# Second block's attention scores: split queries and keys in three single passes on each head's own rows

## The chip, the core and the metric

The kernel runs on one core of one Trainium2 chip. The metric is the device time of one execution in microseconds (us); three runs of the kernel before are given, and their median is the time compared. The engines are TensorE (PE, and PEld for its weight loads), VectorE (DVE), ScalarE (ACT), GpSimd (POOL), and SyncE (SP), which issues the DMAs.

## What is computed

A network of two layers of a first block and two layers of a second block acts on 256 tokens of width 1024, all in float32. The change concerns the second block. There a layer normalises its input, multiplies it by one large matrix, and gives the columns to four kinds of attention with four heads each:

```python
# sparse ("dsa"): an indexer of 8 heads of width 64 chooses the keys, then 4 heads of width 64
dots = jnp.einsum('bthd,bsd->bths', iqb, ik)
score = jnp.einsum('bth,bths->bts', iwb, jax.nn.relu(dots))      # the 64 best keys of a query stay
logits = jnp.einsum('bthd,btjhd->bhtj', qb, k_sel) * scale
# forgetting: 4 heads of width 64, a decay is added to the scores
logits = jnp.einsum('bthd,bshd->bhts', qb, k) * scale + decay
# differential: 4 heads with two score maps each, of width 32; out = (p0 - lam * p1) @ v
logits = jnp.einsum('bthmd,bshmd->bmhts', qb, k) * scale
# sliding: 4 heads of width 64, two key heads, window of 128, a sink in the softmax
logits = jnp.einsum('bnikgd,bnjkd->bnkgij', qb, k_win) * scale
```

Each is causal and followed by a softmax and the product with the values. The four outputs, 1024 columns together, go through an output matrix, a normalisation and a residual sum, and then through a feed-forward part.

## The kernel before, in words

Tokens stand in two tiles of 128. Weights are streamed: `convert` (lines 263 to 298) loads a unit of up to 128x1024 values into `raw`, ScalarE copies it to a high part `wh` of type float32r (line 291), and VectorE, or GpSimd for a few units next to a boundary, subtracts that from `raw` to give the rest `wl` (line 294). `mm3` (line 316) then makes each weight product in three single passes on float32r operands: high by high, high by rest, rest by high (lines 320 to 322). A product of plain float32 operands is one call in the code and two MATMUL instructions in the trace, which are called passes here.

The order of work on each engine is found at build time by a scheduler that simulates the program, and is fixed then; each engine takes its instructions in that order. Where the code puts parts of equal standing by turns, it does so with `weave` (line 540).

A layer of the second block is `second_layer`. Its four mixers `dsa` (1408), `differential` (1532), `sliding` (1585) and `forgetting` (1488) are generators, cut into phases at a bare `yield`. `phases` (551) runs them in the order of `RUN2`: the products of dsa, those of differential, the choosing of dsa, the products of sliding, the attention of differential, the products of forgetting, then the attention of dsa, sliding and forgetting. `BANKS` gives each mixer its two banks of PSUM: `pd` for dsa, `pc` for differential, `pa` for forgetting, `acc` for the attention of sliding; `pt` (181) hands them out by turns. `SLOTS` gives it slots of SBUF of three sizes.

Scores are needed per head, while the transposed queries stand with two heads of width 64 (or four of width 32) on the 128 rows of a tile. The kernel before makes an operand per row position: `padded` (1371) takes two or four tiles [128, 2, 256] and has GpSimd fill them with zeros (line 1379); `pad_copy` (1382) has ScalarE copy only the rows of one position into each (line 1385). The keys stay whole, in one tile (`2_qkT`, or `2_iT` for the indexer), copied by ScalarE at lines 1400, 1493 and 1605. A score is then one float32 matmul on all 128 rows, in which the zeros of the query take the other heads' keys out:

```python
for i, h in enumerate(heads):
    nc.tensor.matmul(bv[:, i], qT[h % 2][:, h // 2, t * 128:t * 128 + 128], kT[:, h // 2, :nk], ...)
```

These stand at line 1445 (indexer, in `choose`), 1479 (dsa), 1525 (forgetting), 1568 (differential) and 1617 (sliding). Queries of tile 0 see 128 keys, those of tile 1 see 256, so a score has 128 or 256 columns.

`softmax_av` (578) takes a token tile's four heads in two steps. A step takes one bank, has `scores` fill it for two heads (first the causal mask as a bfloat16 matmul, `causal_mm`, line 636, and in forgetting the decays as float32 matmuls, lines 1522 and 1524; then the scores), takes the maximum on VectorE (line 590), the negative of it (596), and the exponentials with their sums on ScalarE (601); then it yields to the other token tile. After both steps `av` transposes the probabilities (622), copies them (625, 627) and multiplies by the values (633). The first block's attention (`mixer_c`, scores at line 940) uses the same function. One place of the first block, line 1088, has matmuls on 64 of the 128 rows. The mixed outputs are split into high and rest at lines 383 and 384.

Of the kernel before, what the change touches and what calls it, by code (L numbers as in the profile page):

```python
# [11 lines left out]
F = mybir.dt.float32  # L12
# [9 lines left out]
D = 1024  # L22
# [25 lines left out]
# steps of the two token tiles between two products  # L48
# [53 lines left out]
# work slots of a group: (tag, bytes of a partition, count), the smallest that fits is taken  # L102
# [7 lines left out]
# work tiles and banks of the mixers of the second block, in phase one and two  # L110
# [8 lines left out]
# banks of PSUM of a group  # L119
# [11 lines left out]
class K:  # L131
# [57 lines left out]
    def z(self, shape, name, g=None, dt=F, bufs=None):  # L189
        """work tiles of a group of slots"""  # L190
# [16 lines left out]
    def col_load(self, ap, rows, name):  # L207
        """[rows * 128] contiguous values -> [128, rows] (value r * 128 + p at [p, r])."""
# [9 lines left out]
    def rsq(self, ssq, n, mul, add, name="rs"):  # L218
        """(ssq * mul + add) ** -0.5"""
# [33 lines left out]
    def head(self, kind):  # L253
        """the next units may take those slots as well, when what is before the boundary is done"""
# [8 lines left out]
    def convert(self, i, stack):  # L263
# [4 lines left out]
        # the last units of a product before a boundary have slots of their own  # L268
# [13 lines left out]
        # next to a boundary the vector engine has the norms to do, and small pieces let those pass  # L282
# [3 lines left out]
        if near and i >= self.near + first:  # L286
            # the norms of the token tiles go ahead
# [28 lines left out]
    def mm3(self, out, a, b, first, last):  # L316
        """out += (ah + al).T @ (bh + bl)"""
# [6 lines left out]
    def tm(self, xT, *blocks, outs=None):  # L324
        """token-major products: each block (key, tiles of rows in a unit, columns) -> its columns of a bank a token tile"""
# [15 lines left out]
    def fm(self, xT, key, out=None):  # L341
        """feature-major product of 256 columns: [128, 2, 256]"""
# [11 lines left out]
    def fm_early(self, xT, key, banks=("acc", "pc"), out=None):  # L354
        """the same by way of a token-major product, which needs one token tile at a time"""
# [18 lines left out]
    def tsplit(self, src, t, hT, lT, k0, nk):  # L374
        """src [128 tokens, nk * 128] -> transposed and split into hT, lT[:, k0:k0 + nk, token tile t]"""
# [14 lines left out]
    def sum_sq(self, a, b, psum=False):  # L390
        """steps: sum of a ** 2 and b ** 2 over 1024 columns, / 1024 + eps, to the power of -1/2"""
# [19 lines left out]
    def warm(self, x, n):  # L411
        """products of no use: the clock of the tensor engine halves when it rests between two products"""
# [8 lines left out]
    def steps(self, accs, post, pre, xT, t, gated=False, out=None):  # L421
        """x += rms norm of the product in PSUM; rms norm of the residual stream, transposed and split. In steps, which
        are numbered, so that those of the two token tiles can be put in order"""
        nc = self.nc
        xs = self.halves(t)
        if gated:
            for hf, x in enumerate(xs):
                sg = self.z([128, 512], "ny")
                nc.scalar.activation(sg, accs[t][hf], AF.Tanh, scale=0.5)
                yield                                   # 0, 3  # L430
                nc.vector.scalar_tensor_tensor(sg, sg, 1.0, post[t][hf], op0=OP.add, op1=OP.mult)
                yield                                   # 1, 4
# [3 lines left out]
                yield                                   # 2, 5  # L436
        elif accs is not None:
            sq = self.sum_sq(*accs[t], True)
            for _ in range(2):
                next(sq)  # L440
                yield                                   # 0, 1
            ys = [self.z([128, 512], "ny", "N") for _ in range(2)]
            nc.vector.tensor_tensor(ys[0], accs[t][0], post[0], OP.mult)
            yield                                       # 2
            next(sq)
            r = self.r
            yield                                       # 3
            nc.vector.tensor_tensor(ys[1], accs[t][1], post[1], OP.mult)
            yield                                       # 4
            for hf, (y, x) in enumerate(zip(ys, xs)):  # L450
# [3 lines left out]
                yield                                   # 5, 6  # L454
# [12 lines left out]
        for hf in range(2):  # L467
# [35 lines left out]
    def big_out(self, xT, key, order=range(8)):  # L503
        """[256, K] @ [K, 1024] -> 2 x 2 banks"""
# [5 lines left out]
    def down(self, accs, steps, first, last):  # L510
        """the last units go one token tile after the other, so that the first is done early"""
# [27 lines left out]
    @staticmethod  # L539
    def weave(*gens):  # L540
        """steps of independent parts in turn"""
# [9 lines left out]
    def phases(gens, order):  # L551
        """each mixer stands in the order once for each of its phases, the first of which are its products"""
# [25 lines left out]
    def softmax_av(self, t, scores, v, scale, sinkrow=None, raw=False):  # L578
        """Steps. scores(bank, heads): fills PSUM [128, 2, nk] of two heads; v(h, kt): [128, 64]; gives (o PSUM, rs).
        Heads of one row position of the tensor engine share a bank."""  # L580
# [4 lines left out]
        for par in range(2):  # L585
# [1158 lines left out]
```

## Time and profile before

| | us |
|---|---|
| median of three runs | 1544.99 |
| lowest, highest run | 1538.86, 1549.9 |
| the profiled execution: span from first to last instruction | 1548.7 |
| its own time | not given apart; of the three runs the nearest is 1549.9 |
| TensorE busy, of the span | 1494.2 |
| VectorE, ScalarE, GpSimd busy | 1007.5, 827.9, 288.0 |

"Busy" counts the time in which at least one instruction of the engine is under way. Matmuls overlap in the trace (the next starts before the last has drained), so what a matmul costs is read from the distance of the starts, not from the duration. A chain row shows, piece by piece, the work that ended last.

### The profile page before, as it was taken

How to read it: one execution, taken by the hardware profiler on the slowest of the kernel's cores; microseconds unless marked ns; L12 is line 12 of the kernel's file. 1: busy time of each engine (PE TensorE's matmuls, PEld its weight loads, DVE VectorE, ACT ScalarE, POOL GpSimd, SP SyncE). 2: the span in 40 equal slices, each digit the busy share in tenths (PEclk: the TensorE clock that was granted, in tenths of full speed). 3: DMA queues.
4: the chain of work that ended last, by engine and by line, in shares of the span. 5: the costliest groups of instructions: out<-in, count | busy, mean ns of one | idle time of the engine just before them, and what ended most of it. 6: DMA issues, size and time to landing. Idle time of an engine off the chain costs nothing.

```text
span 1548.7 us, 25270 instructions
## 1 busy us (share of the span) xinstructions
PE 1494.2 (96%) x9723; PEld 1337.0 (86%) x9731; DVE 1007.5 (65%) x1737; ACT 827.9 (53%) x1443; POOL 288.0 (19%) x377
## 2 busy tenths in 40 slices
PE   7999999999998999999999999999999999999998
PEld 7978889999896887999978888899977888899996
DVE  6897577556789755656666875554566695654455
ACT  5735456445574534544445674555564575555553
POOL 1554210000255322000033122000014231100010
PEclk9999999999999979999999999999999999999999
DMA  7522246666452213666646343556654543466663
GB/s 236 150 84 83 72 149 189 186 183 198 135 158 79 74 57 111 191 188 181 189 135 191 105 138 116 180 187 190 187 188 135 165 124 109 130 190 188 190 194 109
DMA packets 156422, 234.12 MB, mean 151 GB/s; under 512 B 11700, under 2 KB 118158, under 8 KB 156302
## 3 DMA queue, kind: packets, MB, share of 16 engines
q1 hardware_dynamic: 156302, 232.51, 49.5%
q8 instruction: 76, 1.25, 0.3%
q14 instruction: 44, 0.36, 0.1%
HBM read 231.43 MB, written 1.05 MB: 150 GB/s over the span
## 4 chain that ended last, share of the span: by engine, by line
PE 77%; DVE 12%; ACT 4%; DMA 3%; POOL 2%; issue 2%; SPq 0%; ACTq 0%; DVEq 0%; POOLq 0%
PE acc L322 7%; PE acc L320 7%; PE acc L321 7%; PE pa L320 6%; PE pa L322 6%; PE pa L321 6%; PE pc L320 5%; PE pc L322 5%; PE pc L321 5%; PE pd L322 4%; PE pd L321 4%; PE pd L320 4%; DVE wl L294 3%; DVE gl_r L700 1%; ACT wh L291 1%
## 5 line engine op out<-in xcount | busy, mean ns | idle before, releaser
L294 DVE TENSOR_TENSOR wl<-raw,wh 128x1024 fp32r<-128x1024 f32 (+4 forms) x424 | 485.3, 1152 | 362.8 <-ACT wh L291 361.7
L291 ACT ACTIVATE wh<-raw 128x1024 fp32r<-128x1024 f32 (+4 forms) x420 | 433.2, 1035 | 413.2 <-PE pd L321 100.0
L294 POOL TENSOR_TENSOR wl<-raw,wh 128x1024 fp32r<-128x1024 f32 (+1 forms) x26 | 61.7, 2374 | 647.6 <-ACT wh L291 647.6
L322 PE MATMUL pa<-xTh,wl 128*128 128x256 f32 x512 | 145.5, 284 | 0.0
L320 PE MATMUL pa<-xTh,wh 128*128 128x256 f32 x512 | 145.4, 284 | 0.0
L321 PE MATMUL pa<-xTl,wh 128*128 128x256 f32 x512 | 145.2, 284 | 0.0
L322 PE MATMUL pd<-xTh,wl 128*128 128x256 f32 x432 | 122.4, 283 | 0.5 <-DVE wl L294 0.5
L320 PE MATMUL pd<-xTh,wh 128*128 128x256 f32 x432 | 122.3, 283 | 0.0
L321 PE MATMUL pd<-xTl,wh 128*128 128x256 f32 x432 | 122.2, 283 | 0.0
L320 PEld LDWEIGHTS pa<-xTh,wh 128*128 128x128 f32 x512 | 98.2, 192 | 0.3
L321 PEld LDWEIGHTS pa<-xTl,wh 128*128 128x128 f32 x512 | 98.2, 192 | 0.3
L322 PEld LDWEIGHTS pa<-xTh,wl 128*128 128x128 f32 x512 | 98.1, 192 | 0.2
L320 PEld LDWEIGHTS pd<-xTh,wh 128*128 128x128 f32 x432 | 82.8, 192 | 0.9
L321 PEld LDWEIGHTS pd<-xTl,wh 128*128 128x128 f32 x432 | 82.8, 192 | 0.9
L322 PEld LDWEIGHTS pd<-xTh,wl 128*128 128x128 f32 x432 | 82.8, 192 | 0.8 <-DVE wl L294 0.8
L321 PE MATMUL acc<-wl,f_h 128*128 128x512 f32 x200 | 78.4, 392 | 0.0
L322 PE MATMUL acc<-wh,f_l 128*128 128x512 f32 x200 | 77.3, 390 | 0.6 <-DVE f_l L1259 0.6
L321 PE MATMUL pc<-wl,f_h 128*128 128x512 f32 x200 | 77.8, 389 | 0.0
L322 PE MATMUL pc<-wh,f_l 128*128 128x512 f32 x200 | 77.5, 389 | 0.0
L320 PE MATMUL acc<-wh,xTh 128*128 128x512 f32 (+4 forms) x200 | 71.3, 360 | 1.5 <-ACT xTh L477 1.1
L320 PE MATMUL acc<-wh,f_h 128*128 128x512 f32 x200 | 71.4, 393 | 0.2 <-ACT f_h L1257 0.2
L320 PE MATMUL pc<-wh,f_h 128*128 128x512 f32 x200 | 71.3, 389 | 0.0
(630 smaller groups left out, 3869.8 us busy)
## 6 DMA issues: line engine op xcount, KB each, us to landing
raw<-in_w_in_dram SPq DMA_DIRECT2D x84, 512.0 KB, 3.7
raw<-in_w_mlp_up_dram SPq DMA_DIRECT2D x64, 512.0 KB, 3.8
raw<-in_w_mlp_down_dram SPq DMA_DIRECT2D x64, 512.0 KB, 3.7
raw<-in_ffn_w_gate_dram SPq DMA_DIRECT2D x44, 512.0 KB, 3.8
raw<-in_ffn_w_up_dram SPq DMA_DIRECT2D x44, 512.0 KB, 3.8
raw<-in_ffn_w_down_dram SPq DMA_DIRECT2D x44, 512.0 KB, 3.6
raw<-in_w_out_dram SPq DMA_DIRECT2D x32, 512.0 KB, 3.8
raw<-in_w_ple_gate_dram SPq DMA_DIRECT2D x16, 512.0 KB, 4.3
```

Of the source, the lines that this page charges most:

```text
L291: nc.scalar.activation(h[:, p], raw[:, p], AF.Copy)
L294: e.tensor_tensor(l[:, p], raw[:, p], h[:, p].bitcast(F), OP.subtract)
L320: t.matmul(out, ah, bh, start=first, stop=False, skip_group_check=True)
L321: t.matmul(out, ah, bl, start=False, stop=False, skip_group_check=True)
L322: t.matmul(out, al, bh, start=False, stop=last, skip_group_check=True)
L700: nc.vector.tensor_tensor(R[:, j].rearrange("p h (b s) -> p h b s", s=s), ev[:, ft[j], :, 1][:, None].to_broadcast([128, 2, 128 // s, s]), ...
```

## The change

Each set of queries and keys becomes a pair of float32r tiles, high part and rest (`hl`), made by `split_to`: ScalarE copies the high part from PSUM, VectorE subtracts it from the same PSUM values. The padded operands, their zeros and the copies into them go. A score is three single passes, high by high, high by rest, rest by high, on the 64 (or 32) rows of its own head. `softmax_av` takes both banks at once, and `row_mm` issues the passes of two heads on different row positions by turns, one into each bank; both banks are filled before the softmax of the first begins, and there is one yield for the two. In `choose` the eight heads are ordered the same way, and the heads of a row position share a bank. The probabilities are as wide as the keys. Comments were removed too; they are left out of the diff.

```diff
 def softmax_av(self, t, scores, v, scale, sinkrow=None, raw=False):
...
-        for par in range(2):
+        banks = [self.pt()[:, :2 * nk].rearrange("p (h k) -> p h k", k=nk) for _ in range(2)]
+        scores(banks)
+        for par, bv in enumerate(banks):
             hs = slice(par, 4, 2)
-            bv = self.pt()[:, :2 * nk].rearrange("p (h k) -> p h k", k=nk)
-            scores(bv, (par, par + 2))
...
-            Pp = self.z([128, 2, 256], "sm_p")
+            Pp = self.z([128, 2, nk], "sm_p")
...
-            yield
+        yield
...
+    def row_mm(self, banks, q, k, last=True):
+        for j in range(2):
+            qk = [(q(i, j), k(i, j)) for i in range(2)]
+            for n, (x, y) in enumerate(((0, 0), (0, 1), (1, 0))):
+                for bv, (a, b) in zip(banks, qk):
+                    self.nc.tensor.matmul(bv[:, j], a[x], b[y], start=False, stop=last and n == 2 and j == 1,
+                                          skip_group_check=True)
+    def rows_of(self, w, t, nk, q, k):
+        rr = lambda i: slice(i * w, i * w + w)
+        return (lambda i, j: [x[rr(i), j, t * 128:t * 128 + 128] for x in q], lambda i, j: [x[rr(i), j, :nk] for x in k])
+    def hl(self, n, name):
+        return [self.z([128, n, 256], name, dt=FR) for _ in range(2)]
+    def split_to(self, dst, o, src):
+        h, l = dst
+        self.nc.scalar.activation(h[o], src, AF.Copy)
+        self.nc.vector.tensor_tensor(l[o], src, h.bitcast(F)[o], OP.subtract)
...
 def heads_T(self, src, n, dst, t):
...
-            if isinstance(y, list):
-                self.pad_copy(y, p[:, g:g + m], 128 // len(y), ts)
-            else:
-                nc.scalar.activation(y[:, :m, ts], p[:, g:g + m], AF.Copy)
+            self.split_to(dst[g // 2], (slice(None), slice(0, m), slice(t * 128, t * 128 + 128)), p[:, g:g + m])
...
 def dsa(self, l, xT):
-        qT, kT = qkT = [self.padded(64, "2_qz"), self.z([128, 2, 256], "2_qkT")]
-        iT = [self.padded(64, "2_iz"), self.padded(64, "2_iz"), self.z([128, 2, 256], "2_iT")]
+        qT, kT = qkT = [self.hl(2, "2_qT"), self.hl(2, "2_kT")]
+        iT = [self.hl(2, "2_iq"), self.hl(2, "2_iq"), self.hl(1, "2_ik")]
...
 def choose(t):
-            for h0 in range(0, 8, per):
-                hl = [(h0 + i) * 2 % 8 + (h0 + i) // 4 for i in range(per)]
-                p = self.pt().rearrange("p (h k) -> p h k", k=nk)
-                for i, h in enumerate(hl):
-                    nc.tensor.matmul(p[:, i], iT[h // 4][h % 2][:, h // 2 % 2, t * 128:t * 128 + 128], iT[2][:, 0, :nk],
-                                     start=True, stop=True)
+            rr = lambda i: slice(64 * i, 64 * i + 64)
+            for j0 in range(0, 4, per):
+                banks = [self.pt().rearrange("p (h k) -> p h k", k=nk) for _ in range(2)]
+                for j in range(j0, j0 + per):
+                    for n, (x, y) in enumerate(((0, 0), (0, 1), (1, 0))):
+                        for i, p in enumerate(banks):
+                            nc.tensor.matmul(p[:, j - j0], iT[j // 2][x][rr(i), j % 2, t * 128:t * 128 + 128],
+                                             iT[2][y][rr(i), 0, :nk], start=n == 0 and j == j0, stop=n == 2,
+                                             skip_group_check=True)
...
 def scores(banks):          # of dsa; the same in sliding
+                for bv in banks:
...
                     self.causal_mm(bv, t, start=False)
-                for i, h in enumerate(heads):
-                    nc.tensor.matmul(bv[:, i], qT[h % 2][:, h // 2, t * 128:t * 128 + 128], kT[:, h // 2, :nk],
-                                     start=False, stop=i == 1, skip_group_check=True)
+                self.row_mm(banks, *self.rows_of(64, t, nk, qT, kT))
...
 def forgetting(self, l, xT):
-        qT, kT = self.padded(64, "2_qz"), self.z([128, 2, 256], "2_qkT")
-        self.pad_copy(qT, self.fm(xT, ("2bq", l)), 64)
-        nc.scalar.activation(kT, self.fm(xT, ("2bk", l)), AF.Copy)
+        qT, kT = self.hl(2, "2_qT"), self.hl(2, "2_kT")
+        self.split_to(qT, slice(None), self.fm(xT, ("2bq", l)))
+        self.split_to(kT, slice(None), self.fm(xT, ("2bk", l)))
...
 def scores(banks):          # of forgetting: masks and decays of both banks, then
+                self.row_mm(banks, *self.rows_of(64, t, nk, qT, kT))
...
 def differential(self, l, xT):
-        qT, kT = qkT = [self.padded(32, "2_qz"), self.z([128, 2, 256], "2_qkT")]
+        qT, kT = qkT = [self.hl(2, "2_qT"), self.hl(2, "2_kT")]
...
+                    rr = lambda i: slice(32 * (2 * i + m), 32 * (2 * i + m) + 32)
+                    self.row_mm(banks, lambda i, j: [x[rr(i), j, t * 128:t * 128 + 128] for x in qT],
+                                lambda i, j: [x[rr(i), j, :nk] for x in kT])
...
 def sliding(self, l, xT):
-        qT, kT = self.padded(64, "2_qz"), self.z([128, 2, 256], "2_qkT")
+        qT, kT = self.hl(2, "2_qT"), self.hl(2, "2_kT")
...
-            self.pad_copy(qT, p[:, :2], 64, slice(t * 128, t * 128 + 128))
-            nc.scalar.activation(kT[:, :, t * 128:t * 128 + 128], p[:, 2:], AF.Copy)
+            ts = (slice(None), slice(None), slice(t * 128, t * 128 + 128))
+            self.split_to(qT, ts, p[:, :2])
+            self.split_to(kT, ts, p[:, 2:])
```

## Rows read from the trace of the kernel before

**Rows 1.** The page: busy time by engine; chain by engine.

```profile
PE 1494.2 (96%) x9723; PEld 1337.0 (86%) x9731; DVE 1007.5 (65%) x1737; ACT 827.9 (53%) x1443; POOL 288.0 (19%) x377
...
PE 77%; DVE 12%; ACT 4%; DMA 3%; POOL 2%; issue 2%; SPq 0%; ACTq 0%; DVEq 0%; POOLq 0%
```

**Rows 2.** Busy us by stretch: PE, PEld, DVE, ACT, POOL; then clock, DMA, GB/s.

```profile
815.00:860.00 45.00, 45.00 (x254) 39.61 (x253) 30.85 (x46) 25.77 (x42) 12.26 (x10) 1.00 0.67 195
860.00:910.00 50.00, 47.89 (x337) 43.42 (x336) 44.63 (x144) 37.28 (x105) 15.00 (x16) 1.00 0.36 111
...
1187.00:1232.00 45.00, 45.00 (x254) 39.60 (x253) 30.86 (x46) 25.84 (x42) 12.33 (x10) 1.00 0.67 194
1232.00:1282.00 50.00, 48.04 (x340) 43.73 (x339) 44.87 (x146) 36.54 (x106) 15.00 (x16) 1.00 0.38 114
...
870.00:880.00 10.00, 9.85 (x75) 8.97 (x73) 9.77 (x29) 7.19 (x17) 3.15 (x4) 1.00 0.23 59
```

**Rows 3.** Chain in the second stretch: start us, us to the next piece.

```profile
884.79 0.45 PE pc L1568 x4
885.24 0.12 PE pa L321
...
886.32 0.87 PE pc L1568 x4
...
903.45 0.81 ACT sm_p L601 x4
...
909.00 0.44 PE pd L622 x4
```

**Rows 4.** Score lines: passes, duration ns min/median/max, first, last start, forms.

```profile
L1445 PE MATMUL pd<-2_iT,2_iz x64: 272/326/382, 853.5 to 1240.1; 128*128 128x128 f32 x32, 128*128 128x256 f32 x32
...
L1479 PE MATMUL pd<-2_qkT,2_qz x32: 275/327/382, 893.0 to 1272.0; 128*128 128x128 f32 x16, 128*128 128x256 f32 x16
...
L1525 PE MATMUL pa<-2_qkT,2_qz x32: 275/327/382, 906.0 to 1292.6; 128*128 128x128 f32 x16, 128*128 128x256 f32 x16
...
L1568 PE MATMUL pc<-2_qkT,2_qz x64: 275/327/383, 870.2 to 1264.1; 128*128 128x128 f32 x32, 128*128 128x256 f32 x32
...
L1617 PE MATMUL acc<-2_qkT,2_qz x32: 272/327/382, 897.6 to 1282.7; 128*128 128x128 f32 x16, 128*128 128x256 f32 x16
```

**Rows 5.** Timeline of TensorE around line 1088: start us, us.

```profile
82.60 0.60 PE L671 MATMUL pa<-gl_q,b_k 128*128 128x256 f32 x2
83.13 1.13 PE L1088 MATMUL pd<-d_qkT,d_kT 64*128 64x256 f32 x4
84.19 0.50 PE L321 MATMUL pa<-wl,xTh 128*128 128x512 f32 x1
84.52 0.39 PE L322 MATMUL pa<-wh,xTl 128*128 128x512 f32 x1
84.75 0.40 PE L320 MATMUL pa<-wh,xTh 128*128 128x512 f32 x1
...
475.22 1.14 PE L1088 MATMUL pd<-d_qkT,d_kT 64*128 64x256 f32 x8
476.29 0.92 PE L671 MATMUL pa<-gl_q,b_k 128*128 128x256 f32 x3
```

**Rows 6.** Lines of remainders, padded copies and zeros; columns as in rows 4.

```profile
L384 DVE TENSOR_TENSOR mTl<-pd,mTh x6: 412/416/424, 163.6 to 923.3; 128x256 fp32r<-128x256 f32 x6
...
L479 DVE TENSOR_TENSOR mTl<-pd,mTh x6: 681/682/690, 1174.8 to 1520.5; 128x512 fp32r<-128x512 f32 x6
...
L1385 ACT ACTIVATE 2_iz<-pd x16: 359/378/380, 818.8 to 1209.4; 64x256 f32<-64x256 f32 x16
...
L1379 POOL MEMSET 2_qz<- x20: 524/528/533, 808.0 to 1186.1; 128x512 f32 x20
```

**Rows 7.** Waits, 810 to 930 us: total us, times, longest.

```profile
POOL 2_r L962 <- DVE rp L961: 40.6, 7, 15.6
...
PE pd L622 <- ACT sm_p L601: 1.3, 1, 1.3
```

More of the change, by code (lines that the diff above doesn't have):

```diff
@@ L936, in attend, with scores @@
         def attend(t):
-            def scores(bv, heads):
-                self.causal_mm(bv, t)
-                for i, h in enumerate(heads):
-                    nc.tensor.matmul(bv[:, i], qT[t][:, h], kT[h // 2][:, h % 2, :128 * (t + 1)], start=False,
-                                     stop=i == 1, skip_group_check=True)
+            def scores(banks):
+                for par, bv in enumerate(banks):
+                    self.causal_mm(bv, t)
+                    for i in range(2):
+                        h = 2 * i + par
+                        nc.tensor.matmul(bv[:, i], qT[t][:, h], kT[h // 2][:, h % 2, :128 * (t + 1)], start=False,
+                                         stop=i == 1, skip_group_check=True)
             o, rs = yield from self.softmax_av(t, scores, lambda h, kt: V[kt][:, h], 96 ** -0.5)
@@ L1369, in plan_second @@
         self.tail(nxt)
-    def padded(self, w, name):
-        out = [self.z([128, 2, 256], name) for _ in range(128 // w)]
-        with ExitStack() as stack:
-            for g in self.gates.get("pool", ()):
-                stack.enter_context(self.tc.issue_after(g))
-            for y in out:
-                self.nc.gpsimd.memset(y, 0.0)
-        return out
-    def pad_copy(self, dst, src, w, ts=slice(None)):
-        for c, y in enumerate(dst):
-            r = slice(c * w, c * w + w)
-            self.nc.scalar.activation(y[r, :, ts], src[r], AF.Copy)
     def heads_T(self, src, n, dst, t):
@@ L1472, in attend, with scores @@
             sb = sbs[t]
-            def scores(bv, heads):
-                nc.tensor.matmul(bv, self.identb, sb[:, None, :].to_broadcast([128, 2, nk]), start=True, stop=False,
-                                 skip_group_check=True)
-                self.causal_mm(bv, t, start=False)
-                for i, h in enumerate(heads):
-                    nc.tensor.matmul(bv[:, i], qT[h % 2][:, h // 2, t * 128:t * 128 + 128], kT[:, h // 2, :nk],
-                                     start=False, stop=i == 1, skip_group_check=True)
+            def scores(banks):
+                for bv in banks:
+                    nc.tensor.matmul(bv, self.identb, sb[:, None, :].to_broadcast([128, 2, nk]), start=True, stop=False,
+                                     skip_group_check=True)
+                    self.causal_mm(bv, t, start=False)
+                self.row_mm(banks, *self.rows_of(64, t, nk, qT, kT))
             o, rs = yield from self.softmax_av(t, scores, lambda h, kt: V[kt][:, h * 64:h * 64 + 64], 64 ** -0.5)
@@ L1563, in attend, with scores @@
             for m in range(2):
-                def scores(bv, heads):
-                    self.causal_mm(bv, t)
-                    for i, h in enumerate(heads):
-                        hm = 2 * h + m
-                        nc.tensor.matmul(bv[:, i], qT[hm % 4][:, hm // 4, t * 128:t * 128 + 128], kT[:, hm // 4, :nk],
-                                         start=False, stop=i == 1, skip_group_check=True)
+                def scores(banks):
+                    for bv in banks:
+                        self.causal_mm(bv, t)
+                    rr = lambda i: slice(32 * (2 * i + m), 32 * (2 * i + m) + 32)
+                    self.row_mm(banks, lambda i, j: [x[rr(i), j, t * 128:t * 128 + 128] for x in qT],
+                                lambda i, j: [x[rr(i), j, :nk] for x in kT])
                 Ps.append((yield from self.softmax_av(t, scores, None, 32 ** -0.5, raw=True)))
@@ L1609, in attend, with scores @@
             nk = 128 * (t + 1)
-            def scores(bv, heads):
-                self.causal_mm(bv, t)
-                if t:
-                    nc.tensor.matmul(bv[:, :, :128], self.identb, wm[:, None, :].to_broadcast([128, 2, 128]),
-                                     start=False, stop=False, skip_group_check=True)
-                for i, h in enumerate(heads):
-                    nc.tensor.matmul(bv[:, i], qT[h % 2][:, h // 2, t * 128:t * 128 + 128], kT[:, h // 2, :nk],
-                                     start=False, stop=i == 1, skip_group_check=True)
+            def scores(banks):
+                for bv in banks:
+                    self.causal_mm(bv, t)
+                    if t:
+                        nc.tensor.matmul(bv[:, :, :128], self.identb, wm[:, None, :].to_broadcast([128, 2, 128]),
+                                         start=False, stop=False, skip_group_check=True)
+                self.row_mm(banks, *self.rows_of(64, t, nk, qT, kT))
             o, rs = yield from self.softmax_av(t, scores, lambda h, kt: V[kt][:, h // 2 * 64:h // 2 * 64 + 64], 64 ** -0.5,
```

39 lines of the change are left out of this document (20 added, 19 removed).

## The prediction

> **What bounds the kernel now.** I read the page's busy shares and its chain first, then the busy times by stretch for the two mixing stages of the second block, then the chain inside one of them, then the rows of the lines that change. TensorE is busy for 96% of the span and carries 77% of the chain; VectorE carries 12%, ScalarE 4% [rows 1]. The two mixing stages lie at 815 to 925 us and 1187 to 1297 us. In the first 45 us of each, TensorE is full and VectorE has 14 us free; in the 50 us that follow, TensorE is busy for 47.9 us and VectorE for 44.6 [rows 2], so there both are close to full. Inside that stretch the chain still runs from matmul to matmul: score groups of four take 0.45 and 0.87 us in it, with weight products of 0.12 us between them [rows 3], and the wait lists hold only small waits of TensorE for another engine, such as 1.3 us for an exponential [rows 7]. A microsecond off TensorE is therefore worth nearly a microsecond before 860 us, and less after it, where VectorE is next.
>
> **The matmuls that go.** The five score lines issue 64 + 64 + 32 + 32 + 32 = 224 passes (each fp32 product is two), half with 128 columns and half with 256 [rows 4]. Four with 128 columns take 0.45 us on the chain, so 0.112 each; four with 256 take 0.87, so 0.217 each [rows 3]. 112 x 0.112 + 112 x 0.217 = 36.8 us.
>
> **The matmuls that come.** 112 products x 3 single passes = 336, issued as 168 pairs: one pass on the rows of one head, the next on other rows into another bank. No row shows a single pass on part of the rows. For the pace of a pass on all rows there are two: 0.12 us with 256 columns (the weight products), and four passes of 128 columns in 0.44, so 0.11 [rows 3]. For two row positions by turns there is one place: line 1088 has products on 64 rows, and where its two positions happened to be issued by turns, eight passes took 475.22 to 476.29, 1.07 us, as long as four passes on one position alone (83.13 to 84.19, 1.06 us) [rows 5]. So a pair costs what one pass costs there. Taken over: 84 pairs x 0.11 + 84 x 0.12 = 19.3 us. The other end, no overlap of single passes, is 38.6 us. I take 19.3, the nearest row.
>
> A rule speaks for less. The pace of 0.11 us with 128 columns is hardly below the 0.12 with 256 [rows 3]. The Trainium skill (TensorE: Matmul & The Clock Gate, Back-to-back issue gap) gives about 56 ns for an isolated matmul of 128 columns; by that the 84 pairs would cost 4.7 us instead of 9.2, and the sum below would be 4.5 us lower. The row measures twice that figure, so the trace does not agree and the row is used.
>
> **The change of row count.** Going from 128 rows to 64 and back isn't free. At 82.60 two full passes start, which at 0.217 end at 83.03, but the next start is 83.13: 0.10 lost. The four on 64 rows then need 1.06 instead of 0.87: 0.19 lost. The full pass after them takes 84.19 to 84.52, 0.33, where the next takes 0.23: 0.10 lost [rows 5]. One visit costs 0.39 us. The changed code makes 13 groups a layer: three of choose, two each of dsa, forgetting and sliding attention, four of differential. Masks and sums on all 128 rows stand ahead of each score group, so neighbours don't merge: 26 x 0.39 = 10.1 us. Bounds: half of it, 5, if the entry and exit are partly hidden by shorter passes; twice, 20, if weight products cut each group in two. The groups of four of before are uncut, so I keep 10.1.
>
> TensorE in sum: 19.3 + 10.1 - 36.8 = -7.4 us for both layers. Of this, choose gives per layer 16 x 0.112 + 16 x 0.217 = 5.3 against 12 x 0.11 + 12 x 0.12 + 3 x 0.39 = 3.9, so -1.3; and all the rest -2.4 a layer.
>
> **VectorE.** Queries and keys now need a remainder: one copy to the high part on ScalarE, then one subtraction on VectorE. Per layer 10 in dsa, 4 in differential, 2 in forgetting, 4 in sliding. The kernel has the same operation for its mixed operand: 0.42 us for 128x256, 0.68 for 128x512 [rows 6]. 18 x 0.42 (two are only half as wide) + 2 x 0.68 = 8.9 us a layer. Fourteen come before 860 us, 5.9 us against 14.1 free: hidden, and if that cover were gone they would cost up to 5.9. Six (sliding, forgetting) come after 860: 4 x 0.42 + 2 x 0.68 = 3.0. There VectorE would need 44.6 + 3.0 = 47.6 us of a stretch that TensorE, 2.4 us lighter, would like to end in 47.6 [rows 2]. An engine that takes its work in order and waits for others doesn't run without a gap, so I give back half of the gain of this part, 1.2 us a layer, 2.4 in all. The ends: nothing given back (-7.4), or the whole gain and the 3.0 us on top.
>
> **ScalarE and GpSimd.** The copies into padded operands, two or four of some 0.38 us where there is now one, shrink by 15 a layer, 11 us over both layers. ScalarE is off the chain before 860 us (25.8 of 45 us busy [rows 2]), so I count nothing; if it counted, it would be a gain of that size at most. The 28 memsets of 0.53 us (the 20 of one name stand in [rows 6], 8 more are alike) go from GpSimd, which spent 40.6 us of the stage waiting for VectorE [rows 7]: nothing. No DMA is issued or moved.
>
> **The order of the softmax.** A step now fills both banks of its mixer before either is read. The second token tile's group waits until both banks have been read by the exponentials; behind it on TensorE stands whatever the schedule put there, weight products while they last and other mixers' matmuls after. Six such waits a layer; each is worth between nothing (other work placed ahead) and the four pieces of a bank's exponentials, 0.81 us [rows 3], so 0 to 10 us in all. Four mixers and the weight products take turns, so I take nothing and keep the 10 for the range. The first block's attention only gets the new order: nothing. The probabilities of tile 0 take smaller slots: nothing.
>
> **Sum.** -7.4 + 2.4 = -5.0 us. The profiled execution spans 1548.7 us; what lies around the span isn't shown, and I take it as unchanged. It would span 1543.7. It lies 3.7 us above the median of the runs, 1545.0, so on the median's scale the forecast is 1540.0.
>
> **Rivals.**
> *VectorE sets the time after 860 us.* Then TensorE's lead there is worth nothing, the 5.4 us that VectorE still has free are waits that stay, and the 3.0 us of subtractions land on the path: 2 x (3.0 - 1.3) = +3.4, 1548; with all 8.9 on the path 2 x (8.9 - 1.3) = +15.2, 1560. It decides from the point where the weights' remainders (0.12 us passes wait for them) come later than TensorE wants them. For it: 44.6 of 50 us busy, and 9.77 of the 10 from 870 us [rows 2]. Against it: the chain there goes over matmuls [rows 3]. Beside it stands the Trainium skill (TensorEngine Tiling, PSUM Bottleneck): tiling makes TensorE faster but not the reading of PSUM, which may become the bottleneck.
> *All of TensorE's gain is kept, and visits are cheap.* With visits at half price and nothing given back: 19.3 + 5 - 36.8 = -12.5, 1532. For it: the full first 45 us and the chain of matmuls. Against it: the 0.39 is measured.
> *The two positions don't run side by side with single passes, or weight products cut the groups.* The first gives 38.6 + 10.1 - 36.8 = +11.9, 1557; the second 19.3 + 20 - 36.8 = +2.5, 1548. For it: no row shows a single pass on part of the rows, and the overlap was seen once. Against it: that one place is clear.
>
> **How the numbers follow.** Forecast 0.52; VectorE 0.22; full gain 0.13; no overlap or cut groups 0.13. The range runs from 1529 (the full gain and some of the runs' own spread, which is 11 us wide) to 1554 (the VectorE case and part of the last one, leaving out its end). The forecast alone would be 1533 to 1546. About 1%, 15.4 us, is what a measurement of this kernel can tell from no change. Below 1529.5 lies half of the full-gain case and little else, 0.08; above 1560.4 the far ends of the VectorE case, of the waits for both banks and of no overlap, 0.07; between them 0.85.
>
> **What would show it.** Right: score passes starting in pairs nearly together, six pairs in about 0.7 us; a gap of about 0.1 us at each side of a group and a slow first pass; VectorE at 47 us or more in the 50 us after the same point; the second mixing stage shorter by 2 to 3 us from its first weight product to its last mixer matmul. Wrong: passes of a pair 0.11 us apart (no overlap); TensorE idle for microseconds between weight products with a remainder as releaser (VectorE); groups of fewer than twelve passes; or a stage as long as before with TensorE idle where the scores were.

## The result and the profile after

The changed kernel takes 1599.03 us (median of 4 runs, 1593.21 to 1605.55) against 1547.22 beside it: 1.0338 times the time before, 95% interval 1.0296 to 1.0379, so 52 us slower. The forecast was 1540, the range ended at 1554.

The page of the changed kernel: first TensorE's and VectorE's busy time, then the granted clock by fortieth of the span (in tenths, 9 is full), then the chain; to be read beside [rows 1].

```profile
PE 1536.8 (96%) x9843; PEld 1361.4 (85%) x9843; DVE 1023.5 (64%) x1777; ACT 818.2 (51%) x1413; POOL 273.7 (17%) x349
...
PEclk9999899999999989999999789999999979999999
...
PE 76%; DVE 11%; ACT 4%; DMA 4%; POOL 3%; issue 2%; SPq 0%; ACTq 0%; DVEq 0%; POOLq 0%
```

By shares nothing has happened: TensorE is busy for 96% and carries the chain as before. But it is busy for 42.6 us more (1494.2 before), and the row of the clock has a 7 and an 8 side by side at 880 to 960 us and another 7 from 1280, where the second block's mixing stages lie. So the stages come next: each from the last transpose of the norm ahead of it to the first of the norm behind it, busy time by engine, then the granted clock. The kernel before:

```profile
810.00:954.00 144.00, 139.44 (x865) 122.75 (x863) 102.33 (x256) 86.66 (x206) 40.33 (x43) 1.00 0.46 140
1182.00:1325.40 143.40, 139.26 (x864) 122.77 (x863) 101.68 (x251) 85.57 (x204) 40.31 (x43) 1.00 0.47 141
```

The changed kernel, the same two stages, and then four stretches of the first of them:

```profile
811.70:982.00 170.30, 159.77 (x922) 134.09 (x920) 111.04 (x277) 82.07 (x191) 34.62 (x33) 0.91 0.39 119
1210.00:1379.20 169.20, 160.43 (x921) 134.91 (x919) 109.63 (x271) 80.38 (x189) 34.86 (x33) 0.91 0.39 118
...
815.00:862.00 47.00, 47.00 (x272) 41.09 (x271) 33.79 (x59) 21.88 (x34) 13.54 (x9) 1.00 0.64 186
862.00:900.00 38.00, 35.16 (x235) 30.65 (x234) 32.85 (x102) 18.82 (x44) 4.13 (x6) 0.96 0.28 85
...
906.00:922.00 16.00, 16.00 (x71) 12.02 (x70) 11.18 (x30) 10.80 (x34) 6.91 (x8) 0.51 0.28 97
...
940.00:960.00 20.00, 15.36 (x86) 12.56 (x86) 7.64 (x33) 5.78 (x23) 0.00 (x0) 0.85 0.02 3
```

The two stages grew by 339.5 - 287.4 = 52.1 us; all the rest of the span by 1.8. A stage's length is idle time of TensorE (length less busy), plus time lost to the clock (busy times 1 less the clock), plus what its work would take at full clock. Before: 8.7 idle, 0 lost, 278.7 of work. After: 19.3 idle, 320.2 x 0.09 = 28.8 lost, 291.4 of work. So more than half of the loss is a clock that falls to 1.2 GHz: from 906 to 922 us while TensorE has no idle time at all (16.00 of 16.00 busy), and in the tail. This split is the measure for all that follows. The clock is rounded to 0.01, so the loss can be off by 1.6 us; and a split is that of one execution, the profiled one, which can lie some us from the median (e15 below: 1587.57 us, median 1580.35).

The new lines. First the score passes of differential and dsa, then three rows of the subtraction and of who waits for it in both layers (columns as in [rows 4]; the last: total us, times):

```profile
L643 PE MATMUL pc<-2_kT,2_qT x96: 268/275/387, 872.9 to 1305.6; 32*128 32x128 f32 x48, 32*128 32x256 f32 x48
...
L643 PE MATMUL pd<-2_kT,2_qT x48: 271/412/579, 904.7 to 1318.3; 64*128 64x128 f32 x24, 64*128 64x256 f32 x24
```

```profile
L658 DVE TENSOR_TENSOR 2_qT<-pa,2_qT x4: 406/416/424, 880.1 to 1290.4; 128x256 fp32r<-128x256 f32 x4
L658 DVE TENSOR_TENSOR 2_qT<-acc,2_qT x2: 673/674/674, 882.5 to 1280.8; 128x512 fp32r<-128x512 f32 x2
...
  PE acc L320: 5.1, 2
```

The subtractions take what [rows 6] show for the like, 0.42 and 0.67 us; dsa's passes, most of them at the low clock (17 of the 24 of the first stage start after 906.4 us), take 0.41 where differential's take 0.28 (these durations overlap). Now three places of the first stage. TensorE's timeline about 883 us (start, duration; in brackets the idle time before it and what ended that):

```profile
880.46 0.28 PE L322 MATMUL acc<-xTh,wl 128*128 128x256 f32 x1
883.30 0.36 PE L320 MATMUL acc<-wh,xTh 128*128 128x260 f32 x1 [2.56 <-DVE 2_qT L658]
...
884.73 0.88 PE L643 MATMUL acc<-2_kT,2_qT 64*128 64x128 f32 x6
```

VectorE's timeline ahead of it, and a line of ScalarE's:

```profile
878.60 1.23 DVE L294 TENSOR_TENSOR wl<-raw,wh 128x1024 fp32r<-128x1024 f32 x1
879.75 0.42 DVE L1470 MAX8 2_m<-2_sc 128x8 f32<-128x256 f32 x1
880.08 0.41 DVE L658 TENSOR_TENSOR 2_qT<-pa,2_qT 128x256 fp32r<-128x256 f32 x1
...
881.33 0.70 DVE L294 TENSOR_TENSOR wl<-raw,wh 128x520 fp32r<-128x520 f32 x1
881.95 0.61 DVE L1470 MAX8 2_m<-2_sc 128x8 f32<-128x256 f32 x2
882.48 0.67 DVE L658 TENSOR_TENSOR 2_qT<-acc,2_qT 128x512 fp32r<-128x512 f32 x1
...
881.21 0.58 ACT L657 ACTIVATE 2_qT<-acc 128x512 fp32r<-128x512 f32 x1
```

The product of forgetting's queries in `acc` is done at 880.7. Its bank is now read by a subtraction too, which VectorE reaches at 882.48, behind the choosing of keys and a weight's remainder; the next product wants that bank. The copy that the subtraction needs ends at 881.79, so VectorE's queue costs 0.69 us here and the subtraction itself 0.67. TensorE waits 2.56 us (5.1 in both layers), and the clock falls behind that: it is low from 885.9 to 889.3 us.

The second place is the exponentials of sliding attention's first bank, on ScalarE's timeline:

```profile
937.83 0.37 ACT L601 ACTIVATE sm_p<-acc,sm_nb 128x128 f32<-128x128 f32 x1
```

The scores that they read were there at 885.61 (the last row of TensorE's timeline above). Sliding attention's second tile, its values and its output come after that, alone, in the stretch from 940 us in which no engine is full; the output product waits for them.

The third is the score groups. Here two of them, TensorE's timeline:

```profile
896.75 0.27 PE L663 MATMUL pc<-cb 128*128 128x256 bf16 x1
896.95 0.88 PE L643 MATMUL pc<-2_kT,2_qT 32*128 32x128 f32 x6
897.76 0.39 PE L321 MATMUL pa<-wl,xTh 128*128 128x260 f32 x1
897.98 0.28 PE L322 MATMUL pa<-wh,xTl 128*128 128x260 f32 x1
...
898.91 0.88 PE L643 MATMUL pc<-2_kT,2_qT 32*128 32x128 f32 x6
```

These are the twelve passes of one step, which should alternate: six on one row position, weight products, six on the other. TensorE's issue order shows that of the 168 pairs only some 52 alternate, in 48 groups and not 26 (the trace has 59 cases of two passes that start within 0.02 us of each other): a bank is filled as soon as it is free, and the second one is free later.

### The profile page after: what moved, and what is told of

It reads as the page before. It is cut to its first block, busy times and chain, and to the rows that moved or that the text cites. A ratio compares the mean times of both kernels' runs of the same rounds, so it can differ in the third digit from the quotient of the medians.

```text
span 1602.6 us, 25522 instructions
## 1 busy us (share of the span) xinstructions
PE 1536.8 (96%) x9843; PEld 1361.4 (85%) x9843; DVE 1023.5 (64%) x1777; ACT 818.2 (51%) x1413; POOL 273.7 (17%) x349
## 4 chain that ended last, share of the span: by engine, by line
PE 76%; DVE 11%; ACT 4%; DMA 4%; POOL 3%; issue 2%; SPq 0%; ACTq 0%; DVEq 0%; POOLq 0%
PE acc L320 6%; PE acc L322 6%; PE acc L321 6%; PE pa L320 6%; PE pa L321 6%; PE pa L322 6%; PE pc L320 4%; PE pc L322 4%; PE pc L321 4%; PE pd L322 4%; PE pd L321 4%; PE pd L320 4%; DVE wl L294 2%; ACT wh L291 2%; DVE gl_r L724 1%
```

## Experiments

All runs with their split of the two stages. The last columns are worked out from one row per stage as above.

| kernel | us | ratio to before (interval) | idle | lost to clock | work at full clock |
|---|---|---|---|---|---|
| before | 1547.22 | | 8.7 | 0 | 278.7 |
| changed | 1599.03 | 1.0338 (1.0296-1.0379) | 19.3 | 28.8 | 291.4 |
| e1_bank_by_bank | 1601.12 | 1.0351 (1.0311-1.0391) | 16.4 | 17.2 | 295.8 |
| e2_before_both_banks | 1552.44 | 1.0028 (1.0003-1.0054) | 13.0 | 2.8 | 279.1 |
| e3_all_rows | 1574.16 | 1.0162 (1.0129-1.0194) | 19.8 | 10.3 | 283.3 |
| e4_no_rests | 1580.30 | 1.0225 (1.0194-1.0257) | 16.4 | 18.4 | 286.2 |
| e5_all_rows_no_rests | 1567.09 | 1.0146 (1.0112-1.0180) | 19.3 | 8.8 | 284.2 |
| e7_paired | 1589.43 | 1.0294 (1.0258-1.0330) | 28.7 | 29.1 | 276.9 |
| e8_rests_on_gpsimd | 1590.49 | 1.0283 (1.0236-1.0329) | 18.2 | 30.0 | 285.4 |
| e9_paired_gpsimd | 1596.12 | 1.0323 (1.0282-1.0364) | 34.5 | 25.8 | 277.1 |
| e14_e5_wide_slots | 1549.10 | 1.0012 (0.9994-1.0030) | 7.6 | 1.4 | 282.4 |
| e15_slots_for_sliding | 1580.35 | 1.0218 (1.0190-1.0246) | 8.9 | 25.1 | 289.1 |
| e16_paired_slots | 1569.57 | 1.0159 (1.0124-1.0194) | 15.4 | 22.4 | 276.0 |
| e17_paired_gpsimd_slots | 1577.19 | 1.0189 (1.0152-1.0227) | 22.4 | 17.7 | 275.2 |
| e19_rests_only | 1557.09 | 1.0075 (1.0046-1.0104) | 11.8 | 4.3 | 281.1 |
| e20_rows_only | 1555.00 | 1.0049 (1.0028-1.0069) | 7.4 | 4.3 | 283.8 |
| e21_paired_rows_only | 1564.66 | 1.0112 (1.0082-1.0142) | 19.0 | 11.4 | 273.7 |

The kernel before ran beside each set: 1547.22, 1548.10 (e1 to e4), 1546.81 (e5 to e9), 1547.92 (e14 to e17) and 1548.16 us (e19 to e21).

**First set: is it the order of the softmax, the row passes or the remainders?** At first I blamed the order.

```diff
 # e1: softmax_av of the changed kernel
-        banks = [...]
-        scores(banks)
-        for par, bv in enumerate(banks):
+        for par in range(2):
+            bv = self.pt()[:, :2 * nk].rearrange("p (h k) -> p h k", k=nk)
+            scores(bv, par)
...
-        yield
+            yield
```

`row_mm` of e1 issues the six passes of one bank; the choosing stays as changed.

> The changed kernel with the softmax of before: a step fills one bank with the mask and the six passes of one row position, reads it, yields, and then does the other bank. The split operands, the three passes on 64 or 32 rows and the choosing scores stay as changed. Theory S (the order of the softmax, both banks filled before either is read, lengthens each mixer and leaves sliding attention alone at the end of the stage: some 20 of the 26 us that each mixing stage of the second block grew): 1550 to 1565 us, and the stage ends without a late pair of sliding groups. Theory R (the passes on part of the rows: 24 visits a layer in place of 13, and TensorE's granted clock at 0.50 for some 16 us behind them): 1590 to 1605, as the changed kernel. Theory V (VectorE's remainders come late): 1590 to 1605.

```diff
 # e2: softmax_av of the kernel before
-        for par in range(2):
-            bv = self.pt()[:, :2 * nk].rearrange("p (h k) -> p h k", k=nk)
+        banks = [self.pt()[:, :2 * nk].rearrange("p (h k) -> p h k", k=nk) for _ in range(2)]
+        for par, bv in enumerate(banks):
             scores(bv, (par, par + 2))
+        for par, bv in enumerate(banks):
...
-            yield
+        yield
```

> The kernel before with one edit alone: a softmax step fills both banks with the old zero padded products before either is read, and yields once. No remainders, no passes on part of the rows. Theory S: 1580 to 1600 us, with TensorE waiting near the end of both mixing stages of the second block. Theories R and V: 1540 to 1555, as before.

```diff
 # e3: rows_of, choose and differential of the changed kernel
-        rr = lambda i: slice(i * w, i * w + w)
+        rr = lambda i: slice(None)
```

> The changed kernel with every score pass on all 128 rows of queries and keys, so that the scores of the heads that share these rows are added up: another result, with the same number of passes, the same columns, banks, remainders and softmax order. Theory R: no change of row count and no fall of the clock behind it: 2 x (24 x 0.39 + 8) = 35 us less, 1560 to 1570. Theory S: most passes stood alone on one row position already (0.11 to 0.12 us each in the trace), so only the visits go, and part of these lies in waiting time: 1585 to 1600. Theory V: as changed, 1595 to 1602.

```diff
 # e4: hl and split_to of the changed kernel
-        return [self.z([128, n, 256], name, dt=FR) for _ in range(2)]
+        return [self.z([128, n, 256], name, dt=FR)] * 2
...
-        self.nc.vector.tensor_tensor(l[o], src, h.bitcast(F)[o], OP.subtract)
```

> The changed kernel without VectorE's subtractions: the low part of queries and keys is the high part again, so the three passes multiply high parts only and the scores come out about three times as large. Row passes and softmax order stay. Theory V: the 2.7 us wait of TensorE for a remainder and VectorE's full stretch in the middle of the stage go, 1570 to 1585. Theories S and R: 1590 to 1602.

Theory S fell: without the new order the changed kernel stays at 1601, and the order alone costs the kernel before 4.3 us (0.5 to 8.4 by the interval). In e1 the clock does not fall behind the score groups any more (17.2 us lost for 28.8), but the tail is there and no pass of the four attentions has a partner (295.8 of work). Both other edits help, by 25 and 19 us, and neither brings the time back. The late tail stands in e1, e3 and e4, which have the changed work tiles, and not in e2. In e4, which has no subtraction, TensorE still waits at the place of the 2.56 us, for another instruction of VectorE:

```profile
872.05 0.36 PE L320 MATMUL acc<-wh,xTh 128*128 128x260 f32 x1 [1.65 <-DVE rp L986]
```

So without the subtractions this wait is 0.9 us shorter, and not gone; but behind the 1.65 us the clock does not fall.

**Second set: do the two add up, and can either be mended?** e5 has the edits of e3 and e4. e7 orders the passes:

```diff
 # e7: row_mm; lastmask is the causal mask of the second bank
+        with self.tc.issue_after(self.lastmask):
             for j in range(2):
...
 # e7: choose
+                    for j, n, i in todo:    # i = 1 first
+                        first = nc.tensor.matmul(banks[i][:, j - j0], ...)
+                        if (j, n, i) == todo[0]:
+                            stack.enter_context(self.tc.issue_after(first.ins))
```

```diff
 # e8: split_to
-        self.nc.scalar.activation(h[o], src, AF.Copy)
-        self.nc.vector.tensor_tensor(l[o], src, h.bitcast(F)[o], OP.subtract)
+        f = self.z([128] + list(src.shape[1:]), "2_full")
+        self.nc.scalar.activation(f, src, AF.Copy)
+        self.nc.scalar.activation(h[o], f, AF.Copy)
+        self.nc.gpsimd.tensor_tensor(l[o], f, h.bitcast(F)[o], OP.subtract)
```

> Both of the edits that helped, together: every score pass on all 128 rows (scores of heads added up) and no subtraction on VectorE (the low part is the high part again). What is left of the change is the softmax order, three passes for two, and the high copies. If the row passes (26 us by e3) and the remainders (19 us by e4) are two causes that add up: 1550 to 1560 us, level with before, and TensorE's granted clock stays near 1.00 in both mixing stages. If a third cause holds the time: 1565 to 1575. If the two are one and the same loss, seen twice: about 1574, as e3.

> The changed kernel with an issue order alone: the passes of a score group are queued behind the last mask of its second bank (in choosing, behind the first pass of the second bank), so that they alternate between the two row positions as the change has it written. In the changed kernel's issue order only some 52 of the 168 pairs alternate, in 48 groups; here some 133, in 40. If the row passes cost by their count (passes that stand alone, 0.11 each, and visits of 0.39): 80 x 0.11 + 8 x 0.39 = 12 us less, 1585 to 1590. If they cost by the clock that falls behind them (0.50 for some 16 us a stage): as long as before or longer, 1595 to 1605, with the clock at 0.50 behind the score groups again.

> The changed kernel with the remainders taken off VectorE and off the banks: ScalarE copies queries and keys to SBUF whole, makes the high part from that copy, and GpSimd subtracts. A weight product's bank is free after one ScalarE copy. Theory V (the subtraction stands in VectorE's queue behind the choosing of keys, and TensorE waits for the bank that it reads): 1575 to 1588, as with no subtractions. If what counts is the length of the chain from the product to the score operands, which this makes longer: 1600 to 1615.

> e7 and e8 together, which computes the reference in full. If the causes add up (12 us and 15 to 19 us): 1568 to 1575; still slower than before, as the fall of the clock behind the row passes stays. If pairing moves nothing: as e8, 1575 to 1588. A version faster than before, under 1540, only if the clock stays at 1.00 too.

e5 stayed at 1567, 20 us above before, with 19.3 us idle: there was a third cause. e7 did to TensorE's work what the change is written to do, 291.4 to 276.9. A group of it, TensorE's timeline:

```profile
887.54 0.28 PE L664 MATMUL pc<-cb 128*128 128x256 bf16 x1
887.75 0.89 PE L644 MATMUL pc<-2_kT,2_qT 32*128 32x128 f32 x12
888.56 0.39 PE L321 MATMUL pa<-wl,xTh 128*128 128x260 f32 x1
```

Twelve passes take 0.81 us, 887.75 to 888.56, as long as the six at 896.95 in the changed kernel (to 897.76). But idle time rose by 9.4 us, and the time fell by only 10. A group now waits for its second bank by the way it is issued; the longest waits of TensorE that are new in a stage are 2.2 us at a decay of forgetting (line 1538, for VectorE's maximum) and 2.3 us at a transpose (622, for VectorE's work on the sink), so the later softmax counts too. e8 gave 9 us, less than expected; with pairing (e9) nothing was left of it.

**Third set: the work slots.** The change made the probabilities of tile 0 half as wide. Work slots are picked by size, so sliding attention's went from the 2 KB slots to the 1 KB slots that it shares with differential attention.

```diff
 # e14: on e5
-            Pp = self.z([128, 2, nk], "sm_p")
+            Pp = self.z([128, 2, 256], "sm_p")
...
 # e15: on the changed kernel (e16: on e7, e17: on e9)
-            Pp = self.z([128, 2, nk], "sm_p")
+            Pp = self.z([128, 2, nk], "sm_p", "N" if self.g == "e2" else None)
```

> e5_all_rows_no_rests (score passes on all 128 rows, low part the same as the high part) with one edit: the probabilities of the first token tile are 256 wide again, so they go back to the work slots of 2 KB that they had before the change, where the change puts them into the 1 KB slots that sliding attention shares with differential attention. Theory T (sliding's first exponentials wait until differential attention is done with a 1 KB slot, in the changed kernel until 937.8 us for scores that are there at 885.6, and this makes the late tail of the stage): 1548 to 1556 us, no late sliding groups, clock 1.00. If the tail comes from the order of the softmax: 1565 to 1570, as e5.

> The changed kernel, whole, with one edit: sliding attention's probabilities take the 2 KB slots of the norms, which nothing uses in the mixing stage. Theory T: the tail of both stages goes (idle time from about 10 to 6 us a stage, and the fall of the clock behind it, 4 us a stage): 1575 to 1588. Rival (order of the softmax, or the row passes, make the tail): 1594 to 1604, as the changed kernel. The fall of the clock behind the row passes, 8 us a stage, stays under both.

> e15 with the issue order of e7 (passes alternating between the two row positions). Theory T: in e7 TensorE's own work in the two stages was already as short as before (278 against 279 us), and 50 us were idle time and low clock; the part of these in the tail goes: 1565 to 1578. If pairing makes TensorE wait for second banks whatever the slots are: 1582 to 1590.

> e16 with the remainders on GpSimd as in e9. Theory V alone (VectorE's queue holds the bank): 5 to 15 us below e16. If GpSimd's remainders only lengthen the chain, as e9 against e7 (7 us more): 3 to 10 us above e16. Faster than before only if the clock stays at 1.00 through both stages, which no run with row passes has shown so far.

All of it as theory T has it: e14 is level with before, and e15 takes 18.7 us off the changed kernel by one argument. The two differ: e14 gives all four mixers the slots of before back and takes 18.0 us off e5; e15 gives sliding attention, for both of its tiles, slots that nothing else uses there. Sliding attention's exponentials on ScalarE's timeline of e15, to be read beside 937.83 above:

```profile
888.12 0.37 ACT L601 ACTIVATE sm_p<-acc,sm_nb 128x128 f32<-128x128 f32 x1 [0.57 <-DVE sm_nb L594]
```

They come 50 us earlier, and the idle time of the stages is that of before (8.9 for 8.7). e17 came out 8 us above e16, as its second theory had it: on GpSimd the remainders only lengthen the chain.

**Fourth set: what is left, one by one.** e19 is e3, e20 is e4, e21 is e7 without the subtraction, each with the slots of e15.

> e3_all_rows with sliding attention's probabilities in the norms' slots as in e15: remainders on VectorE, but every score pass on all 128 rows (scores of heads added up). What this lies above before is the price of the remainders: the wait of some 2.6 us a stage for a bank, the low clock behind it (3.5 us a stage), and three full passes for two. Expected 1556 to 1562 if the row passes are the larger part; 1570 to 1575 if the remainders are. In the 20 us behind 900 us, where e15's clock falls to 0.50, it should stay at 1.00 here, as the issue order is nearly that of e15.

> e4_no_rests with the same slots: passes on part of the rows, as the schedule orders them, and no remainders (the low part is the high part again). What this lies above before is the price of the row passes: 24 visits a layer, passes that stand alone, and the low clock behind them (8 us a stage). Expected 1564 to 1572 if they are the larger part and add up with e19 to the 32 us of e15; 1553 to 1558 if the remainders are the larger part.

> e20 with the alternating issue order of e7 and e16. If alternating passes alone could pay: TensorE's own work in the stages is then no longer than before (278 us in e7 and e16), so 1545 to 1552 with the clock at 1.00; if the clock falls behind the row passes also here, some 8 us a stage: 1558 to 1566. No theory has it below 1540.

The remainders alone cost 8.9 us, the row passes alone 6.8; both together 32.4 (e15 against before). Each of these has the three passes and the new order of the softmax as well; e14, which has those and neither of the two, costs 1.2. They don't add up, and the clock is why: e15 loses 25.1 us to it, e19 and e20 4.3 each, and 25.1 - 8.6 = 16.5, as much as 32.4 - 15.7 = 16.7. (By the stage lengths of the profiled executions the excess is 35.7 - 9.8 - 8.1 = 17.8 us: 16.5 of clock, 2.9 of work, 1.6 less of idle time.) With the old slots there is an excess as well: against e5 the remainders cost 7.1 (e3), the row passes 13.2 (e4), both 31.9. Stretches of e15 that show it (columns as above):

```profile
896.00:907.00 11.00, 11.00 (x85) 9.57 (x84) 6.60 (x15) 7.11 (x20) 0.00 (x0) 1.00 0.61 204
907.00:927.00 20.00, 20.00 (x87) 15.37 (x86) 12.28 (x44) 12.76 (x46) 7.06 (x8) 0.51 0.20 73
```

e19 issues the same instructions in the same order on every engine in these stages, its score passes on all rows; it stands 5 us earlier:

```profile
902.00:922.00 20.00, 19.58 (x166) 18.81 (x166) 16.95 (x53) 18.82 (x67) 7.95 (x10) 1.00 0.33 116
```

With the same order and the same passes, 87 matmuls are started in 20 us at 1.2 GHz against 166 at 2.4: the partial rows alone make the clock fall here. They don't do so everywhere, nor for as long. In e1, which issues every pass of the four attentions alone, on partial rows and with remainders, the clock stays at 1.00 through the score groups:

```profile
890.00:944.00 54.00, 52.11 (x370) 44.46 (x368) 35.16 (x104) 33.39 (x107) 9.65 (x12) 1.00 0.33 108
```

In e20, whose order is another one since nothing waits for remainders (84 pairs start together, 47 in e15), it came back:

```profile
886.00:895.00 9.00, 9.00 (x71) 7.48 (x69) 7.25 (x21) 8.11 (x21) 0.00 (x0) 1.00 0.67 210
895.00:899.00 4.00, 4.00 (x26) 3.37 (x24) 2.05 (x12) 4.00 (x20) 3.35 (x6) 0.57 0.13 47
899.00:912.00 13.00, 13.00 (x96) 11.14 (x94) 11.26 (x37) 11.11 (x40) 3.92 (x5) 1.00 0.34 100
```

Why the clock stays low for 20 us in one order, for 4 in another and not at all in e1's is open.

Two things stay open. e4, e5, e14, e20 and e21 keep no low parts, so each mixer also holds fewer work tiles; what that gives is not priced apart from the subtractions, though e19's waits for the bank, 2.8 us a stage, are more than the idle time that it has over before (3.1 in both). And no run has the mended slots with the banks one by one, so what the new order of the softmax costs in the whole change stays open.

e21 went against the expectation that pairing helps: its work is the least of all, 273.7 us, and it is 9.7 us slower than e20, with 11.6 us more of idle time and 7.1 more of low clock. The longest of its new waits are those of transposes (line 622) for exponentials, 2.7 and 1.0 us a stage; that they come from the wait for the second bank is likely and not shown.

## Why the prediction was wrong, point by point

- *"The probabilities of tile 0 take smaller slots: nothing."* The step that failed by most: 18.7 us (e15). I looked at the size of the tile and not at who else uses the slots of that size.
- **The clock.** The sum had no term for it, since the clock was at 1.00 in every row of before. It is 28.8 of the 52 us: a consequence, but of waits (2.56 us at 883, the tail) and of partial rows (e15 against e19), so each of these cost more than its own length.
- **The matmuls that come.** *"a pair costs what one pass costs"* held wherever passes alternate (12 in 0.81 us). That they alternate did not: some 52 pairs of 168. The other 116 cost a pass more, 116 x 0.115 = 13.3 us.
- **The visits.** The price held: around the group at 896.95 the mask takes 0.20 us to the next start where a full pass takes 0.12, the six passes 0.81 where six at 0.11 are 0.66, and the pass behind them 0.22 for 0.12: 0.33 lost, near the 0.39. The Trainium skill (TensorEngine Tiling (Array Packing), Key Properties) says that a change of the tiling mode drains TensorE; the 0.33 us lost here fit that. *"13 groups a layer"* was 24: 22 x 0.39 = 8.6 us more. With the point above -7.4 becomes +14.5; measured were 291.4 - 278.7 = +12.7. With alternating passes e7, e16 and e21 measured -1.8, -2.7 and -5.0: so part of the -7.4 was to be had, but not with the order that the schedule gives.
- **VectorE.** The remainders were sized right and priced as time on VectorE. *"Fourteen come before 860 us, 5.9 us against 14.1 free: hidden"* held: two of them came at 867 and 869 us, and TensorE waited for none. The step that failed is the next one, *"Six (sliding, forgetting) come after 860"*, priced at 2.4 us for both layers: one of these six holds a bank that TensorE wants, in a queue that runs in order, and the clock falls behind the wait. 8.9 us for the remainders by themselves (e19). The rival had the engine right and the mechanism wrong: VectorE is not fuller than in [rows 2] (32.85 of 38 us from 862, 86%, against 89%), it is late at one place. The Trainium skill (TensorEngine Tiling (Array Packing), PSUM Bottleneck) says that tiling speeds up TensorE and not the reading of PSUM, which may become the bottleneck. Here it did at one bank, by the length of the reading (0.58 us on ScalarE, then 0.67 on VectorE) and by the reader's place in its queue (0.69).
- **The order of the softmax.** *"0 to 10 us in all"*, taken as nothing: 4.3 us (e2). Right in mechanism: in e2 TensorE waits 3.3 us a stage at dsa's masks (line 1476) until the exponentials have read the banks. In the paired kernels idle time grows by more, 6.5 us in e16 over e15 and 11.6 in e21 over e20, but there the order of issue differs too.
- **ScalarE, zeros, first block: nothing.** Right: ScalarE's busy time fell by 9.7 us (827.9 to 818.2), and the rest of the span moved by 1.8 (over all the kernels here it lies between 1251 and 1267 us, 1261 before).

The causes of the 52 us are then: slots 19; remainders 9; row passes 7; and 17 more where these two meet, through the clock. Part of the 17 can be the order of work, which is another in e20 than in e15. The new order of the softmax is no item of its own: e14 has it too, and is level with before. That the range ended at 1554 came from the first two points, neither of which stood among the bounds.

Two of the signs of being wrong that the prediction named came: groups of fewer than twelve passes, and TensorE idle with a remainder as releaser.

No version here beats the kernel before. At best the work saved is 278.7 - 273.7 = 5 us in both stages (e21, which leaves the remainders out; 3.5 with them, e17), and each way to it costs more in waits and clock.

## What to carry to other kernels

When a tile changes its size, look up which pool it moves to and who holds that pool, before calling it free; in a full schedule a slot is a wait. When an engine is added as a reader of a bank, price the wait of whoever needs the bank next, in the order of that engine's queue. And read idle time, granted clock and work at full clock apart for the stage: a busy share of 96% can hide all three.

## What was not expected of the hardware

TensorE's clock fell to 1.2 GHz while TensorE was never idle (20.00 of 20.00 us busy in e15, clock 0.51), among passes on 64 and 32 rows; the same order on 128 rows kept 1.00 (e19), and so did passes on 64 and 32 rows in another order (e1, 890 to 944 us). Single passes on two row positions by turns run fully beside each other: 12 in the 0.81 us of 6 (e7).
